# One written order of the seven products in the gate and up stage, with the fourth product cut in halves around the fifth

## The chip, the cores and the metric

The kernel runs on one core of one Trainium2 chip. The metric is device time in microseconds (us) of one execution of the whole program. TensorE multiplies, VectorE and ScalarE work element by element, and SyncE issues the DMAs. Each engine has its own list of instructions and takes them strictly in the order of that list; a semaphore makes an instruction wait for one of another engine.

## The reference, cut to what matters

The reference is one inference step of a one-layer decoder: input projection, windowed attention and pooling, output projection with a layer norm, and a gated feed-forward part. The change touches the gate and up products of the last part alone:

```python
def post_sublayers(h, attn_out, pool_out, w_o, ln1_g, ln1_b, w_gate, w_up, w_down, ln2_g, ln2_b):
    mix = jnp.einsum('bte,ed->btd', jnp.concatenate([attn_out, pool_out], -1), w_o)
    h1 = layer_norm(DEEPNORM_ALPHA * h + mix, ln1_g, ln1_b)
    a = jax.nn.silu(jnp.einsum('btd,df->btf', h1, w_gate)) * jnp.einsum('btd,df->btf', h1, w_up)
    ff = jnp.einsum('btf,fd->btd', a, w_down)
    return layer_norm(DEEPNORM_ALPHA * h1 + ff, ln2_g, ln2_b)
```

All is float32. There are 520 tokens here (8 sample rows and 512 prompt rows), 2048 model columns and 5632 feed-forward columns, which are 44 tiles of 128.

## The kernel before

**Seven products for a pair of tiles.** The gate and up stage works on 22 pairs of feed-forward tiles, and for each pair first on the gate weights (the "gate set", `g8` for pair 8), then on the up weights (the "up set", `u8`). A set has four raw weight tiles of 128x1024: two feed-forward tiles by two halves of the model columns. The 2x2 block product is done with seven products in place of eight (a Strassen-Winograd scheme). Products 1, 2 and 4 take a raw tile as it is; 7, 6, 5 and 3 take a *weight sum*, made in place by VectorE (line 196, one operation over 128x1024). The sums follow from each other: that for P6 needs the one for P7, those for P5 and P3 need the one for P6.

**Halves.** float32 precision is made of two float32r operands. Each 128x1024 tile is cut into two *halves* of 512 columns (P4a and P4b are the halves of P4). For each half `split` makes a *high part* (a cast on ScalarE, line 187) and a *low part* (a subtraction on VectorE, line 188). Then TensorE does 12 matmuls of 128x260 for it: four blocks of 128 columns, by three matmuls each (lines 203 and 204 read the high part, line 206 the low part). A full product is 24 matmuls.

**The ring.** High and low parts lie in two rings of five slots (`WB = 5`, line 46, set in line 810). Slots are given out in the order in which the code calls `split`: a half takes the slot of the half that was written five calls earlier, and its cast waits until TensorE has read that one.

**Accumulators.** P1, P6, P5 and P3 add up in one PSUM bank (`p1_g8`, `al` in the code), P7 and P4 in a second (`p7_g8`, `ga`), P2 has a third (`p2_g8`, `de`). Between the products of a bank its running value is copied out or added to the output rows (lines 1018 to 1054), and the next product on that bank waits for that reader.

**Filled, kept and other sets.** In ten early up sets (u1 to u11 without u5) P1 has been made beforehand, outside of the ring ("filled", `p1`). In g0 and u0 both P1 and P2 have been made ("kept"). All other sets do seven products. The written order in `run` (lines 1007 to 1061) depends on this: filled sets write P7, P2, P6, P4, P5, P3; kept ones P7, P6, P4, P5, P3; the others P1, P7, P6, P2, P5, P4, P3.

**What sets the order on the engines.** A scheduling pass of the framework places every instruction by its dependences, priorities and its own estimate of times; the written order decides which slot of the ring and which raw tile a half gets, and is the pass's starting point, but it does not fix the order on an engine. `weight_sum` (line 193) adds one fixed edge: a sum stands on VectorE behind the low part that was written last. The raw tiles (line 177) come by DMA from SyncE into six slots, each load as soon as the last reader of the slot is done. While gate set i runs, the results of pair i-1 are prepared for the next stage by `staged` (lines 1091 to 1116: four adds and eight casts and subtractions, with DMAs to `t_d`); `next(side)` places its pieces between the products.

Of the kernel before, what the change touches and what calls it, by code (L numbers as in the profile page):

```python
# [67 lines left out]
def hybrid_step(ctx, tc, xin, w_in, w_o, w_g, w_u, w_d, w_pool, par_d, cst_d, ident_d, ln2gb, kct_d, vc_d, hist_d,  # L68
                ck_d, cv_d, sp_d, yp, ys, nkp, nvp, npp, nks, nvs, nps):
    nc = tc.nc  # L70
# [5 lines left out]
    class Region:  # L76

        def __init__(self, name, dt, w):
            self.t, self.dt, self.spare = sb.tile([P, w], dt, name=name), dt, [(0, w)]
# [72 lines left out]
    def row_tile(name, w=NTOK):  # L152

        return ap_.tile([P, NTOK], F32, tag="row", name=name, bufs=bufs["row"])[:, :w]
# [28 lines left out]
    def split(s, name, lo=None):  # L183

        wh, wl = [sp[0].tile(list(s.shape), F32R, tag=t, bufs=sp[1]) for t in ("wh", "wl")]
        with tc.high_priority(prio[0]):
            nc.scalar.copy(wh, s)  # L187
            last_lo[0] = (lo or nc.vector).tensor_sub(wl, s, wh.bitcast(F32)).ins  # L188
        return wh, wl
# [10 lines left out]
    def products(out, wh, wl, hi, lo, first, last, onto=False):  # L200

        for j, o in enumerate(out):
            nc.tensor.matmul(o, wh, hi[j], start=first, stop=False, skip_group_check=onto)  # L203
            nc.tensor.matmul(o, wh, lo[j], start=False, stop=False, skip_group_check=onto)  # L204
        for j, o in enumerate(out):
            nc.tensor.matmul(o, wl, hi[j], start=False, stop=last, skip_group_check=onto)  # L206
# [48 lines left out]
    with ExitStack() as sa:  # L255
# [185 lines left out]
        for h in range(2):  # L441
            for g in range(4):
                n = h * 4 + g + 1
# [244 lines left out]
        def sample_attention():  # L688
# [10 lines left out]
            nc.scalar.copy(sT.rearrange("p j n -> p (j n)"), st_.rearrange("p j t b -> p (j t b)"))  # L699
            prod = pa.tile([P, 8, NS], F32, tag="smp", name="prod")  # L700
            nc.vector.tensor_add(prod, qd[:, 0], qd[:, 1])
            for i in range(2):
                ts = slice(4 * i, 4 * i + 4)
# [111 lines left out]
    def bank(name, w=HN):  # L815
        return ps.tile([P, 512], F32, tag="bank", name=name, bufs=banks)[:, :w]
# [130 lines left out]
    class Set:  # L947


        def __init__(self, w, i, name):  # L950
            self.w, self.i, self.name = w, i, name
            self.raw, self.bk, self.p1, self.s3, self.next = {}, {}, None, False, None

        def q(self, r, c):
            if (r, c) not in self.raw:
# [10 lines left out]
            self.s((1, 0), (0, 0), (1, 0), nc.vector.tensor_sub)  # L966
            self.s3 = True

        def prod(self, n, bk, first=True):


            b = {1: "b11", 2: "b21", 3: "b22", 4: "t4", 5: "t1", 6: "t2", 7: "t3"}[n]
            src = {1: lambda: self.q(0, 0), 2: lambda: self.q(0, 1), 4: lambda: self.q(1, 1),
                   7: lambda: self.q(1, 0) if self.s3 else self.s((1, 0), (0, 0), (1, 0), nc.vector.tensor_sub),
                   6: lambda: self.s((1, 0), (1, 1), (1, 0), nc.vector.tensor_sub),
                   5: lambda: self.s((0, 0), (1, 0), (0, 0), nc.vector.tensor_add),
                   3: lambda: self.s((0, 1), (0, 1), (1, 0), nc.vector.tensor_sub)}[n]()
            for g in range(2):
                wh, wl = split(src[:, g * 512:(g + 1) * 512], f"{self.name}_{n}{g}")
                if g == 0 and n == 1:  # L980
                    self.early()
                if g == 0 and n == 3 and self.next and (self.next.p1 is not None or self.next.bk):

                    self.next.early()
                for kk in range(4):
                    k = 4 * g + kk
                    sl = slice(kk * P, (kk + 1) * P)
                    hi, lo = bop[b][k // 2]
                    products([bk], wh[:, sl], wl[:, sl], [hi[:, k % 2, :]], [lo[:, k % 2, :]], k == 0 and first, k == 7, True)
# [17 lines left out]
        def run(self, c11, c12, c21, c22, side=(), out=None):  # L1007

            side = iter(side)
            r = row_tile(f"p_{self.name}")  # L1010
            filled = self.p1 is not None
            al, de = [self.bk.get(n) for n in (1, 2)]
            if not filled:
                self.p1 = r[:, HALF[0]]
                if al is None:
                    al = bank(f"p1_{self.name}")
                    self.prod(1, al)
                nc.scalar.copy(self.p1, al)
            else:
                al = bank(f"p1_{self.name}")  # L1020
            ga = bank(f"p7_{self.name}")
            next(side, None)
            self.prod(7, ga)
            next(side, None)
            kept = de is not None
            if filled and not kept:
                de = bank(f"p2_{self.name}")
                self.prod(2, de)
            if filled:
                nc.vector.tensor_add(c22, ga, self.p1)  # L1030
            else:
                nc.scalar.copy(c22, ga)
            self.prod(6, al, filled)
            next(side, None)
            if filled:
                nc.vector.tensor_add(c21, al, self.p1)
            else:
                nc.scalar.copy(c21, al)
            if filled or kept:
                self.prod(4, ga, False)  # L1040
            else:
                de = bank(f"p2_{self.name}")
                self.prod(2, de)
            next(side, None)
            nc.vector.tensor_add(c11, de, self.p1)
            if out:
                out(0)
            self.prod(5, al, False)
            next(side, None)
            nc.vector.tensor_add(c22, c22, al)  # L1050
            if not (filled or kept):
                self.prod(4, ga, False)
            next(side, None)
            nc.vector.tensor_add(c21, c21, ga)
            if out:
                out(1)
            self.prod(3, al, False)
            if filled:
                nc.vector.tensor_add(c12, al, self.p1)
                return c12  # L1060
            return al
# [68 lines left out]
    for j, s in enumerate(sets[NKEEP + 1::2][:NFILL]):  # L1130
        if j % 2 == 0:
            f = pb.tile([P, 2, HN], F32, tag="fill", name=f"fill{j}", bufs=NF)
# [82 lines left out]
    def column_pair(c, j):  # L1215

        A = {(r, b): wd[c, j, r, b] for r in range(2) for b in range(2)}
        tri = ps.tile([P, 3, 512], F32, tag="tri", name=f"tri{c}_{j}", bufs=2)[:, :, :HN]
        ga, de, al = [tri[:, i, :] for i in range(3)]
        ac = acc4[j]  # L1220
        if c == 0:
            for r in range(2):
                h = ac[:, 2 * r:2 * r + 2, :]
                nc.scalar.activation(h, h, AF.Copy, scale=ALPHA)

        def prod(n, bk, src, first=True):
            wh, wl = split(src, f"d{c}_{j}_{n}")
            for k in range(KP):
                hi, lo = ops[c][n][k][:, 0, :], ops[c][n][k][:, 1, :]
                products([bk], wh[:, k, :], wl[:, k, :], [hi], [lo], k == 0 and first, k == KP - 1, True)  # L1230

        def add(t, a, b, op):
            weight_sum(op, A[t], A[a], A[b])
            return A[t]


        prod(1, al, A[0, 0])
        yield
# [25 lines left out]
    g, before = [column_pair(0, j) for j in range(2)]  # L1264
# [5 lines left out]
    for x, (c, j) in enumerate(pairs[2:], 2):  # L1270
        g = column_pair(c, j)
# [4 lines left out]
        for i in range(5):  # L1276
# [7 lines left out]
            elif j < 2 * len(PLAIN) and i == 0:  # L1284
# [3 lines left out]
                f = j  # L1288
# [233 lines left out]
```

## Time and profile before

The three timed runs took 1931.68, 1930.22 and 1931.51 us. The page of the profiled execution gives its span and no other time of it.

| what | value |
|---|---|
| median of three runs | 1931.51 us |
| span of the profiled execution | 1931.1 us |
| mean granted TensorE clock | 0.992 |
| gate and up stage, 591 to 1449 us | 858.0 us, TensorE busy 850.15, VectorE 732.52, ScalarE 446.45, DMA share 0.49 |
| down stage, first part, 1449 to 1865 us | 416.0 us, TensorE busy 411.84, VectorE 348.27, ScalarE 172.63, DMA share 0.57 |

The stages' numbers come from the view of busy time by stretch. In the rows PE is TensorE, PEld its weight loads, DVE is VectorE, ACT is ScalarE, SPq the queue of SyncE. In a group's row stand the line, the engine, the operation, what is written and read, the count, the busy time with the mean of one, and the idle time ahead of it with what ended most of it. In the view by time a row gives the start in us, the duration in us and, in brackets, how long the engine was idle and who released it. Matmul records have a duration of 0.28 us but start every 0.12 us, since they are pipelined; starts are what to read there.

### The profile page before, as it was taken

How to read it: one execution, taken by the hardware profiler on the slowest of the kernel's cores; microseconds unless marked ns; L12 is line 12 of the kernel's file. 1: busy time of each engine (PE TensorE's matmuls, PEld its weight loads, DVE VectorE, ACT ScalarE, POOL GpSimd, SP SyncE). 2: the span in 40 equal slices, each digit the busy share in tenths (PEclk: the TensorE clock that was granted, in tenths of full speed). 3: DMA queues.
4: the chain of work that ended last, by engine and by line, in shares of the span. 5: the costliest groups of instructions: out<-in, count | busy, mean ns of one | idle time of the engine just before them, and what ended most of it. 6: DMA issues, size and time to landing. Idle time of an engine off the chain costs nothing.

```text
span 1931.1 us, 39334 instructions
## 1 busy us (share of the span) xinstructions
PE 1894.4 (98%) x15533; PEld 1865.8 (97%) x15533; DVE 1539.9 (80%) x2734; ACT 944.1 (49%) x1808; POOL 2.7 (0%) x9
## 2 busy tenths in 40 slices
PE   9999999999999999999999999999999999999996
PEld 8999999999989999999999999999999999999996
DVE  6666667768777888888888888888877888888878
ACT  6644445545654544554455555555554444344341
POOL 0000000000000000000000000000000000000000
PEclk9999999999999999999999999999999999999998
DMA  8732222665744555454545445454469664645332
GB/s 276 233 101 66 71 78 75 211 202 193 250 150 164 160 160 172 142 162 158 175 139 178 141 138 165 146 167 145 164 212 356 214 221 162 223 163 202 94 99 89
DMA packets 145241, 319.28 MB, mean 165 GB/s; under 512 B 14288, under 2 KB 66232, under 8 KB 144952
## 3 DMA queue, kind: packets, MB, share of 16 engines
q1 hardware_dynamic: 144480, 315.71, 49.7%
q8 instruction: 122, 2.00, 0.4%
q10 hardware_dynamic: 576, 1.05, 0.2%
q14 instruction: 63, 0.52, 0.1%
HBM read 265.22 MB, written 54.03 MB: 165 GB/s over the span
## 4 chain that ended last, share of the span: by engine, by line
PE 92%; DVE 4%; ACT 2%; DMA 1%; issue 1%; SPq 0%; DVEq 0%; ACTq 0%
PE p_g L203 7%; PE p_g L204 7%; PE p_g L206 7%; PE p_u L203 7%; PE p_u L206 7%; PE p_u L204 7%; PE tri L203 7%; PE tri L206 7%; PE tri L204 7%; PE o L203 3%; PE o L206 3%; PE o L204 3%; PE p_u L996 2%; PE mm_u L203 2%; PE mm_u L206 2%; PE mm_u L204 2%
## 5 line engine op out<-in xcount | busy, mean ns | idle before, releaser
L187 ACT CAST rr<-fr 128x512 fp32r<-128x512 f32 (+1 forms) x1056 | 658.0, 643 | 776.6 <-DVE fr L196 224.0
L188 DVE TENSOR_TENSOR rr<-fr,rr 128x512 fp32r<-128x512 f32 (+1 forms) x1056 | 738.0, 717 | 264.5 <-ACT rr L187 253.2
L196 DVE TENSOR_TENSOR fr<-fr 128x1024 f32<-128x1024 f32 (+1 forms) x304 | 319.7, 1052 | 5.8 <-DMA fr<-in_w_g_dram 5.0
L203 PE MATMUL p_g<-rr 128*128 128x260 f32 x830 | 235.5, 285 | 7.4 <-ACT rr L187 7.1
L206 PE MATMUL p_g<-rr 128*128 128x260 f32 x830 | 230.6, 282 | 0.0
L204 PE MATMUL p_g<-rr 128*128 128x260 f32 x788 | 221.8, 282 | 0.0
L203 PE MATMUL p_u<-rr 128*128 128x260 f32 x770 | 217.5, 283 | 0.2 <-ACT rr L187 0.2
L206 PE MATMUL p_u<-rr 128*128 128x260 f32 x770 | 215.3, 282 | 0.0
L204 PE MATMUL p_u<-rr 128*128 128x260 f32 x748 | 210.6, 282 | 0.0
L206 PE MATMUL tri<-rr 128*128 128x260 f32 x696 | 196.8, 283 | 1.5 <-DVE rr L188 1.5
L203 PE MATMUL tri<-rr 128*128 128x260 f32 x696 | 197.0, 283 | 0.7 <-ACT rr L187 0.7
L204 PE MATMUL tri<-rr 128*128 128x260 f32 x696 | 196.7, 283 | 0.0
L203 PEld LDWEIGHTS p_g<-rr 128*128 128x128 f32 x830 | 156.2, 188 | 9.9 <-ACT rr L187 9.4
L206 PEld LDWEIGHTS p_g<-rr 128*128 128x128 f32 x830 | 155.2, 189 | 0.0
L204 PEld LDWEIGHTS p_g<-rr 128*128 128x128 f32 x788 | 148.1, 188 | 0.0
L203 PE MATMUL o<-rr 128*128 128x260 f32 x512 | 145.0, 284 | 0.3 <-ACT rr L187 0.3
L203 PEld LDWEIGHTS p_u<-rr 128*128 128x128 f32 x770 | 144.9, 188 | 0.3 <-ACT rr L187 0.3
L206 PEld LDWEIGHTS p_u<-rr 128*128 128x128 f32 x770 | 144.6, 189 | 0.0
L204 PE MATMUL o<-rr 128*128 128x260 f32 x512 | 144.1, 282 | 0.0
L206 PE MATMUL o<-rr 128*128 128x260 f32 x512 | 143.6, 282 | 0.2 <-DVE rr L188 0.2
L204 PEld LDWEIGHTS p_u<-rr 128*128 128x128 f32 x748 | 140.6, 188 | 0.0
L206 PEld LDWEIGHTS tri<-rr 128*128 128x128 f32 x696 | 131.3, 189 | 2.2 <-DVE rr L188 2.2
(320 smaller groups left out, 4570.0 us busy)
## 6 DMA issues: line engine op xcount, KB each, us to landing
fr<-in_w_u_dram SPq DMA_DIRECT2D x100, 512.0 KB
fr<-in_w_g_dram SPq DMA_DIRECT2D x90, 512.0 KB
fr<-in_w_d_dram SPq DMA_DIRECT2D x64, 640.0 KB
t_d<-fr SPq DMA_DIRECT2D x140, 260.0 KB
fr<-in_w_o_dram SPq DMA_DIRECT2D x64, 512.0 KB
fr<-in_w_in_dram SPq DMA_DIRECT2D x48, 512.0 KB
rr<-t_d SPq DMA_DIRECT2D x87, 260.0 KB
mid_b<-t_d SPq DMA_DIRECT2D x53, 260.0 KB
```

Source lines behind the costliest of these rows:

```text
L187: nc.scalar.copy(wh, s)
L188: last_lo[0] = (lo or nc.vector).tensor_sub(wl, s, wh.bitcast(F32)).ins
L196: i = op(*args).ins
L203: nc.tensor.matmul(o, wh, hi[j], start=first, stop=False, skip_group_check=onto)
L204: nc.tensor.matmul(o, wh, lo[j], start=False, stop=False, skip_group_check=onto)
L206: nc.tensor.matmul(o, wl, hi[j], start=False, stop=last, skip_group_check=onto)
L996: nc.tensor.matmul(bk, self.q(0, n - 1)[:, k * P:(k + 1) * P], z1[0][4 * (n - 1) + k // 2][:, k % 2, :], start=(k == 0), stop=(k == 7))
```

## The change

`run` has one order for all sets: P1 (where it is not made beforehand), P7, P2, P6, the first half of P4, P5, the second half of P4, P3. `source(n)` gives a product's weights and makes the weight sum where one is needed, once; `prod` calls it, and `run` calls it for P5 ahead of P4a and for P3 ahead of P4b, so that these sums are written ahead of the halves. No instruction is added or dropped: the same matmuls, casts, subtractions, sums, adds and loads.

```diff
+        def source(self, n):
+            if n not in self.made:
+                self.made[n] = {
+                    1: lambda: self.q(0, 0), 2: lambda: self.q(0, 1), 4: lambda: self.q(1, 1),
...
+                    5: lambda: self.s((0, 0), (1, 0), (0, 0), nc.vector.tensor_add),
+                    3: lambda: self.s((0, 1), (0, 1), (1, 0), nc.vector.tensor_sub)}[n]()
+            return self.made[n]
+
+        def prod(self, n, bk, first=True, halves=(0, 1)):
...
-            for g in range(2):
+            src = self.source(n)
+            for g in halves:
                 wh, wl = split(src[:, g * 512:(g + 1) * 512], f"{self.name}_{n}{g}")
...
             self.prod(7, ga)
             next(side, None)
-            kept = de is not None
-            if filled and not kept:
+            if de is None:
                 de = bank(f"p2_{self.name}")
                 self.prod(2, de)
...
             self.prod(6, al, filled)
...
-            if filled or kept:
-                self.prod(4, ga, False)
-            else:
-                de = bank(f"p2_{self.name}")
-                self.prod(2, de)
+            self.source(5)
+            self.prod(4, ga, False, (0,))
             next(side, None)
             nc.vector.tensor_add(c11, de, self.p1)
             if out:
                 out(0)
             self.prod(5, al, False)
             next(side, None)
             nc.vector.tensor_add(c22, c22, al)
-            if not (filled or kept):
-                self.prod(4, ga, False)
+            self.source(3)
+            self.prod(4, ga, False, (1,))
             next(side, None)
             nc.vector.tensor_add(c21, c21, ga)
             if out:
                 out(1)
             self.prod(3, al, False)
```

What the scheduling pass makes of it is shown at three places of pair 8. Line numbers above 949 are larger by 3 to 7 in the changed file (1038 there is 1032 before, 1044 is 1038, 1053 is 1050, 1115 is 1112).

**First place: TensorE and ScalarE at P4 of g8.** On TensorE before, behind the last matmuls of P6 (bank `p1_g8`), two matmuls of P4a (bank `p7_g8`) stand ahead of P5 (again `p1_g8`); the other ten come after P5:

```order
L203 MATMUL p1_g8_9125<-rr_61 128x260
L204 MATMUL p1_g8_9125<-rr_61 128x260
L206 MATMUL p1_g8_9125<-rr_61 128x260
L203 MATMUL p7_g8_9158<-rr_61 128x260
L204 MATMUL p7_g8_9158<-rr_61 128x260
L203 MATMUL p1_g8_9125<-rr_61 128x260
L204 MATMUL p1_g8_9125<-rr_61 128x260
L206 MATMUL p1_g8_9125<-rr_61 128x260
```

On TensorE now, all twelve of P4a follow P6 at once, and two of P4b stand ahead of P5. These rows are the end of the twelve, the two, and the start of P5:

```order
L204 MATMUL p7_g8_9158<-rr_61 128x260
L206 MATMUL p7_g8_9158<-rr_61 128x260
L203 MATMUL p7_g8_9158<-rr_61 128x260
L204 MATMUL p7_g8_9158<-rr_61 128x260
L203 MATMUL p1_g8_9125<-rr_61 128x260
L204 MATMUL p1_g8_9125<-rr_61 128x260
L206 MATMUL p1_g8_9125<-rr_61 128x260
```

ScalarE before, from the copy of P1's result to that of P6's (line 1038). The casts of line 187 are those of P7b, P2b, P6a and P6b; then P4b and P5a; then P5b and P4a; then P3a:

```order
L1018 COPY fr_60<-p1_g8_9125 128x260
L187 CAST rr_61<-fr_60 128x512 x4
L1032 COPY fr_60<-p7_g8_9158 128x260
L187 CAST rr_61<-fr_60 128x512 x2
L1111 CAST fr_60<-fr_60 128x520
L187 CAST rr_61<-fr_60 128x512 x2
L1038 COPY fr_60<-p1_g8_9125 128x260
L187 CAST rr_61<-fr_60 128x512
```

ScalarE now, from the same copy of P1's result (line 1025). The casts are P6a, P6b and P4a; then P5a and P5b; then P4b; then P3a, P3b and the first three of u8:

```order
L1025 COPY fr_60<-p1_g8_9125 128x260
L187 CAST rr_61<-fr_60 128x512 x3
L1038 COPY fr_60<-p7_g8_9158 128x260
L1114 CAST fr_60<-fr_60 128x520
L187 CAST rr_61<-fr_60 128x512 x2
L1114 CAST fr_60<-fr_60 128x520
L187 CAST rr_61<-fr_60 128x512
L1070 ACTIVATE fr_60<-fr_60 128x260
L1044 COPY fr_60<-p1_g8_9125 128x260
L187 CAST rr_61<-fr_60 128x512 x5
```

P4a's cast moved from the second last of the set's middle to right behind P6's. Counted in the order of TensorE, P4a's slot was before that of P6b, the half directly ahead of it; now it is that of a half five places ahead.

**Second place: VectorE from P6 to P3 of g8.** Before, from P6b's low part (the first row; line 188 is a low part, 196 a sum, 1097 to 1112 are pieces of `staged`) up to the row ahead of the add that P3 waits for (line 1050). The sums are those for P3 and for P7 of u8; the one for P5 stands ahead of the piece:

```order
L188 TENSOR_TENSOR rr_61<-fr_60,rr_61 128x512
L1098 TENSOR_TENSOR fr_60<-fr_60 128x260
L188 TENSOR_TENSOR rr_61<-fr_60,rr_61 128x512
L196 TENSOR_TENSOR fr_60<-fr_60 128x1024
L188 TENSOR_TENSOR rr_61<-fr_60,rr_61 128x512
L1045 TENSOR_TENSOR fr_60<-p2_g8_9226,fr_60 128x260
L1101 TENSOR_TENSOR fr_60<-fr_60 128x260
L1112 TENSOR_TENSOR fr_60<-fr_60 128x520
L188 TENSOR_TENSOR rr_61<-fr_60,rr_61 128x512 x3
L196 TENSOR_TENSOR fr_60<-fr_60 128x1024
L1112 TENSOR_TENSOR fr_60<-fr_60 128x520
L188 TENSOR_TENSOR rr_61<-fr_60,rr_61 128x512
```

VectorE now, from P6b's low part on (the first row). The sums are those for P5, P3 and P7 of u8; the add of line 1053 that P3 waits for stands directly behind the last row:

```order
L188 TENSOR_TENSOR rr_61<-fr_60,rr_61 128x512
L196 TENSOR_TENSOR fr_60<-fr_60 128x1024
L188 TENSOR_TENSOR rr_61<-fr_60,rr_61 128x512
L1104 TENSOR_TENSOR fr_60<-fr_60 128x260
L1115 TENSOR_TENSOR fr_60<-fr_60 128x520
L1048 TENSOR_TENSOR fr_60<-p2_g8_9191,fr_60 128x260
L188 TENSOR_TENSOR rr_61<-fr_60,rr_61 128x512 x2
L196 TENSOR_TENSOR fr_60<-fr_60 128x1024
L1115 TENSOR_TENSOR fr_60<-fr_60 128x520
L188 TENSOR_TENSOR rr_61<-fr_60,rr_61 128x512 x2
L196 TENSOR_TENSOR fr_60<-fr_60 128x1024
L188 TENSOR_TENSOR rr_61<-fr_60,rr_61 128x512
```

P4a's low part moved ahead of P5's, P4b's behind the sum for P3, and the sum for P5 moved from ahead of P6a's low part to behind P6b's.

**Third place: VectorE at the start of g8.** Before, from the sum for P7 on (P1a's low part is the row ahead): P1b's low part, then the add on u7's bank (line 1050), then P7a's low part:

```order
L196 TENSOR_TENSOR fr_60<-fr_60 128x1024
L188 TENSOR_TENSOR rr_61<-fr_60,rr_61 128x512
L1050 TENSOR_TENSOR fr_60<-fr_60,p1_u7_8940 128x260
L188 TENSOR_TENSOR rr_61<-fr_60,rr_61 128x512
L1081 TENSOR_TENSOR fr_60<-fr_60 128x520
```

VectorE now:

```order
L188 TENSOR_TENSOR rr_61<-fr_60,rr_61 128x512
L196 TENSOR_TENSOR fr_60<-fr_60 128x1024
L1053 TENSOR_TENSOR fr_60<-fr_60,p1_u7_8940 128x260
L188 TENSOR_TENSOR rr_61<-fr_60,rr_61 128x512
L1084 TENSOR_TENSOR fr_60<-fr_60 128x520
```

The add on u7's bank moved ahead of P1b's low part. On TensorE P3 of u7, which waits for it, moved from behind P1 and two matmuls of P7 to behind P1a and two matmuls of P1b, 12 matmuls earlier.

More of the change, by code (lines that the diff above doesn't have):

```diff
@@ L951, in __init__ @@
             self.w, self.i, self.name = w, i, name
-            self.raw, self.bk, self.p1, self.s3, self.next = {}, {}, None, False, None
+            self.raw, self.bk, self.p1, self.s3, self.next, self.made = {}, {}, None, False, None, {}
         def q(self, r, c):
@@ L967, in early @@
             self.s3 = True
-        def prod(self, n, bk, first=True):
-            b = {1: "b11", 2: "b21", 3: "b22", 4: "t4", 5: "t1", 6: "t2", 7: "t3"}[n]
[L973 to L977, printed above, removed]
-            for g in range(2):
+        def source(self, n):
+            if n not in self.made:
+                self.made[n] = {
+                    1: lambda: self.q(0, 0), 2: lambda: self.q(0, 1), 4: lambda: self.q(1, 1),
+                    7: lambda: self.q(1, 0) if self.s3 else self.s((1, 0), (0, 0), (1, 0), nc.vector.tensor_sub),
+                    6: lambda: self.s((1, 0), (1, 1), (1, 0), nc.vector.tensor_sub),
+                    5: lambda: self.s((0, 0), (1, 0), (0, 0), nc.vector.tensor_add),
+                    3: lambda: self.s((0, 1), (0, 1), (1, 0), nc.vector.tensor_sub)}[n]()
+            return self.made[n]
+        def prod(self, n, bk, first=True, halves=(0, 1)):
+            b = {1: "b11", 2: "b21", 3: "b22", 4: "t4", 5: "t1", 6: "t2", 7: "t3"}[n]
+            src = self.source(n)
+            for g in halves:
                 wh, wl = split(src[:, g * 512:(g + 1) * 512], f"{self.name}_{n}{g}")
```

## The prediction

> **What bounds the kernel now.** First the page: its busy times, the shares of the chain that ended last, and the group of the stage that idles most (line, engine, operation; busy us and mean ns; idle us ahead of it).
>
> ```profile
> PE 1894.4 (98%) x15533; PEld 1865.8 (97%) x15533; DVE 1539.9 (80%) x2734; ACT 944.1 (49%) x1808; POOL 2.7 (0%) x9
> PE 92%; DVE 4%; ACT 2%; DMA 1%; issue 1%; SPq 0%; DVEq 0%; ACTq 0%
> L203 PE MATMUL p_g<-rr 128*128 128x260 f32 x830 | 235.5, 285 | 7.4 <-ACT rr L187 7.1
> ```
>
> TensorE is the bound, so time is only to be had from its idle gaps. Of those, the matmuls of the gate sets hold 7.4 us, nearly all ended by a cast. The same stage by stretches (start and end, length, busy time and instructions of TensorE, its weight loads, VectorE, ScalarE, GpSimd, then granted clock, DMA share, GB/s):
>
> ```profile
> 591.00:700.00 109.00, 107.42 (x889) 106.66 (x888) 92.30 (x144) 54.54 (x102) 0.00 (x0) 1.00 0.50 160
> 700.00:800.00 100.00, 98.07 (x812) 97.45 (x811) 87.46 (x142) 51.40 (x96) 0.00 (x0) 1.00 0.51 157
> 800.00:900.00 100.00, 98.55 (x817) 97.96 (x816) 87.74 (x142) 49.15 (x93) 0.00 (x0) 1.00 0.47 151
> 900.00:1000.00 100.00, 98.07 (x812) 97.45 (x811) 87.29 (x143) 50.39 (x95) 0.00 (x0) 1.00 0.53 166
> 1000.00:1100.00 100.00, 99.36 (x828) 99.15 (x828) 86.17 (x135) 53.70 (x101) 0.00 (x0) 1.00 0.48 154
> 1200.00:1300.00 100.00, 100.00 (x836) 100.00 (x835) 87.40 (x137) 54.31 (x103) 0.00 (x0) 1.00 0.50 158
> ```
>
> The last row is TensorE at its limit: 836 matmuls in 100 us, 0.1196 us from start to start (a half of 12 takes 1.435, a product 2.87). At that rate the 889, 812, 817, 812 and 828 matmuls of the first five rows need 106.3, 97.1, 97.7, 97.1 and 99.0 us. The stretches are longer by 2.65, 2.87, 2.27, 2.87 and 0.96: **11.6 us** in all. (A start-to-start count is used because a matmul's record of 0.28 us hides part of a gap.) Where it goes, in TensorE's rows by time in pair 8, the last matmul of P6b, the two of P4a, the first two of P5a:
>
> ```profile
> 862.38 0.28 PE L206 MATMUL p_g<-rr 128*128 128x260 f32 x1
> 863.31 0.39 PE L203 MATMUL p_g<-rr 128*128 128x260 f32 x1 [0.64 <-ACT rr L187]
> 863.53 0.28 PE L204 MATMUL p_g<-rr 128*128 128x260 f32 x1
> 863.65 0.32 PE L203 MATMUL p_g<-rr 128*128 128x260 f32 x1
> 863.81 0.28 PE L204 MATMUL p_g<-rr 128*128 128x260 f32 x1
> ```
>
> From 862.38 to 863.81 are four steps, 0.48 us at full rate, and 1.43 went by: 0.95 lost. ScalarE's rows say why:
>
> ```profile
> 861.19 0.62 ACT L187 CAST rr<-fr 128x512 fp32r<-128x512 f32 x1 [0.36 <-PE p_g L204]
> 862.63 0.62 ACT L187 CAST rr<-fr 128x512 fp32r<-128x512 f32 x1 [0.83 <-PE p_g L204]
> ```
>
> The second cast is P4a's. It stood idle 0.83 us until TensorE had read the slot's former half, and that half is P6b, directly ahead in TensorE's order. Two matmuls of P4a head the queue, so P5a, whose cast and low part were long done, waits behind them. The summary of what TensorE waits for between 591 and 1449 us counts 11 such waits (us in all, times, longest):
>
> ```profile
> PE p_g L203 <- ACT rr L187: 7.1, 11, 0.6
> PE p_g L203 <- ACT fr L1038: 0.3, 1, 0.3
> PE p_u L203 <- ACT rr L187: 0.2, 1, 0.2
> ```
>
> 11 × 0.95 = 10.4 of the 11.6 us. The rest, 1.2, is the other two rows and small steps.
>
> **The change: the bubble.** In the order now, P4a reuses the slot of a half five places ahead, P4b of one three places ahead, and the two matmuls pulled ahead of P5a are P4b's. No half of the changed file reuses the slot of the one directly ahead. With three places, the slot is free two halves (2.87 us) ahead of need, against a release to the cast of 0.25 (862.38 to 862.63), the cast's 0.62 and some 0.06 to the matmul. So all 11 bubbles go: −10.4. No instruction is added.
>
> **The other 1.2 us.** The largest is a VectorE add that P5 of an up set waits for (two rows of TensorE, one of VectorE):
>
> ```profile
> 844.74 0.28 PE L206 MATMUL p_u<-rr 128*128 128x260 f32 x1
> 845.19 0.36 PE L203 MATMUL p_u<-rr 128*128 128x260 f32 x1 [0.16 <-ACT rr L187]
> 844.62 0.42 DVE L1036 TENSOR_TENSOR fr<-p_u,fr 128x260 f32<-128x260 f32 x1
> ```
>
> The add ends at 845.04 and P5 starts 0.15 later: the bracket's cast is not the real releaser. Between P6 and P5 stands P4, as before, but the add has moved ahead of the piece of the stage's results; I count 0.8 us of room in place of 0.3 short. I take −1.2; the bounds are 0 and −1.2.
>
> **VectorE in a gate set.** It now carries the sums for P5 and P3 in the middle. Its prices:
>
> ```profile
> 860.67 1.22 DVE L196 TENSOR_TENSOR fr<-fr 128x1024 f32<-128x1024 f32 x1
> 861.81 0.69 DVE L188 TENSOR_TENSOR rr<-fr,rr 128x512 fp32r<-128x512 f32 x1
> 862.41 0.42 DVE L1045 TENSOR_TENSOR fr<-p_g,fr 128x260 f32<-128x260 f32 x1
> 862.75 0.42 DVE L1101 TENSOR_TENSOR fr<-fr 128x260 f32<-128x260 f32 x1
> 863.09 0.70 DVE L1112 TENSOR_TENSOR fr<-fr 128x520 fp32r<-128x520 f32 x1
> 863.70 1.90 DVE L188 TENSOR_TENSOR rr<-fr,rr 128x512 fp32r<-128x512 f32 x3
> ```
>
> From start to start a sum takes 1.14, a low part 0.60, a short add 0.34, a piece of 128x520 0.61. From P6a's low part to the end of the add that P3 waits for (line 1053) the order has eight low parts (4.8), three sums (3.4), three short adds (1.0), two pieces (1.2) and that add (0.42): 10.9, with the release 11.05. TensorE has 74 matmuls from P6's start to P3's, 8.85 us. So VectorE must be 2.2 us ahead when P6 starts. It can be: P2's last cast waits for TensorE to leave P3 of the set before, 58 matmuls (6.94) ahead of P6; a cast, a low part, a sum and three adds (0.62+0.60+1.14+1.02 = 3.4) leave a lead of 3.5. Margin 1.3, cost 0. With that cover gone, each missing 0.1 would cost 1.1 us in 11 sets.
>
> [...]
>
> **The tight place.** Behind each of the ten filled up sets, P3 moved forward, behind P1a and two matmuls of P1b of the next set, and its add waits on VectorE behind P1a's low part and a sum. Counted from the start T of P5a: P5a's last matmul starts at T+1.32, release 0.25 and cast 0.62 to T+2.19, low part to 2.79, sum to 3.93, add 0.42 and release 0.15 to **T+4.50**. TensorE reaches P3 after 38 matmuls, at **T+4.545**. The margin is nil. The row values scatter by a tenth, so I take 0.05 on average, 10 × 0.05 = +0.5; the bounds are 0 and 0.60 each (one low part placed in between), that is 0 and +6. In sets not filled ten more matmuls stand ahead of P3, and the margin is 1.2.
>
> **The load for P2 of an up set.** P2 now comes ahead of P6 there. SyncE's issue of its raw tile, and the cast that waited for it:
>
> ```profile
> 865.37 0.42 SPq L180 DMA_DIRECT2D fr<-in_w_u_dram  x1
> 871.63 1.14 ACT L187 CAST rr<-fr 128x512 fp32r<-128x512 f32 x2 [3.12 <-DMA fr<-in_w_u_dram]
> ```
>
> 6.26 us pass from issue to cast. The load waits for P5b's low part, now some 2.45 after P6's start in the gate set, in SyncE's order behind two stores as before but ahead of the other load it used to follow. First half cast by 2.45+6.26+0.62 = 9.3; use after 98 matmuls, 11.7. Hidden, by 2.4. If another transfer added over 2.4, each up set would pay the excess.
>
> **What stays.** A gap of 0.9 at the passage to the down stage stays: its cast waits for TensorE's own last reading.
>
> ```profile
> 1448.40 0.28 PE L206 MATMUL p_u<-rr 128*128 128x260 f32 x1
> 1449.43 0.39 PE L203 MATMUL tri<-rr 128*128 128x260 f32 x1 [0.74 <-ACT rr L187]
> ```
>
> Sum: −10.4 − 1.2 + 0.5 = −11.1. The profiled span, 1931.1, is 0.4 under the median of the runs, 1931.5, so the forecast is made against the latter: **1920.4 us**.
>
> **Rivals.** *Half given back.* In the tight place one VectorE operation too many, or its add regularly late by a low part: 10 × 0.60 = 6.0 returned, 1931.5−11.6+6.0 = 1925.9. For it: no margin; against it: the order has nothing else between.
>
> *The bubble only moves* (also: the change doesn't do what it says). The pass has again pulled two matmuls ahead of P5a, now P4b's, and the ring still has five slots. P4b's cast stands behind a piece on ScalarE (line 1114) that needs VectorE. If that cast is late by what P4a's was, 11 × 0.95 comes back: 1931.5−1.2 = 1930.3. For it: the same queue and the same two matmuls; against it: a slot free 2.87 us earlier. The Trainium skill, page "Perfetto Trace Analysis", section "Optimization Strategy", takes regular gaps of TensorE for too few buffers for the next tile. By that rule alone the unchanged ring would leave the gaps, and the time would be near this rival's; the trace agrees that a slot is what the cast waits for, but the stretch from 1200 us, on the same five slots, has none.
>
> *Slower: VectorE falls behind in the gate sets.* Before, VectorE had little lead at P6 of g8 (its start on P6a's low part, TensorE's first matmul of P6, and, in the view by stretches, the whole pair):
>
> ```profile
> 858.19 0.69 DVE L188 TENSOR_TENSOR rr<-fr,rr 128x512 fp32r<-128x512 f32 x1
> 858.43 0.28 PE L203 MATMUL p_g<-rr 128*128 128x260 f32 x1
> 846.00:884.40 38.40, 37.76 (x315) 37.55 (x314) 33.55 (x56) 19.36 (x37) 0.00 (x0) 1.00 0.50 160
> ```
>
> If the lead stays 0.24 where 2.2 is needed, P3 waits 1.96 in 11 sets: 21.6, and 1931.5−11.6+21.6 = 1941.5. It decides for slower at a lead under 0.8, where 11 × 1.4 outweighs 11.6 and the 3.9 of the bound below. For it: three sums in a row of work, and VectorE busy 33.55 of the pair's 38.40 us, 0.90 when the pair takes 37.4. Against it: a whole pair still fits, VectorE ran 87.40 in the 100 us of full rate above, and nothing in the order holds it back before P6 but the cast reckoned above.
>
> **How the numbers follow.** Forecast 0.66; half given back 0.16; bubble moves 0.10; slower 0.08. The low end is no cost in the tight place and a little of the last gap (1918.8). The high end takes in the second case, with the tight place at its bound and 0.6 unexplained: 1926.5. What is left out is the last two cases, 0.18. "Same" is within 0.2%, 3.9 us, about what a measurement of this kernel can tell: 1927.6 to 1935.4, and the third case lies in it. Faster 0.82, same 0.10, slower 0.08.
>
> **What would show it.** Right: between 591 and 1100 us TensorE makes close to 836 matmuls per 100 us; the row of 11 waits on line 187 by p_g is gone; P4a's cast no longer ends an idle time put down to TensorE. The tight place: a wait of p_u on line 203, with VectorE's line 1053 ending just ahead. Load: a wait of p_u for a cast that itself waited for in_w_u. Slower: p_g's P3 waiting, VectorE without idle time from P6 to P3. Wrong would be the whole sum if TensorE's gaps after P6 in gate sets are as long as before under another name.

## The result, and the profile after

| | median, us | runs | span of the profiled execution |
|---|---|---|---|
| before | 1931.6 | 4, 1930.22 to 1931.93 | 1931.1 |
| changed | 1922.42 | 4, 1920.50 to 1923.03 | 1921.2 |

The ratio is 0.995, with a 95% interval of 0.9939 to 0.9962: faster, by 9.2 us (7.3 to 11.8 by the interval). Inside the stage the profile shows more. The view of busy time by stretch of the changed kernel, in the columns of the prediction's table:

```profile
591.00:700.00 109.00, 109.00 (x909) 108.94 (x908) 94.56 (x149) 57.29 (x105) 0.00 (x0) 1.00 0.49 164
700.00:800.00 100.00, 100.00 (x836) 100.00 (x835) 89.99 (x146) 54.05 (x99) 0.00 (x0) 1.00 0.50 159
800.00:900.00 100.00, 100.00 (x837) 100.00 (x835) 88.80 (x146) 53.65 (x98) 0.00 (x0) 1.00 0.53 170
900.00:1000.00 100.00, 100.00 (x837) 100.00 (x836) 89.07 (x145) 52.32 (x95) 0.00 (x0) 1.00 0.49 159
1000.00:1100.00 100.00, 100.00 (x837) 100.00 (x837) 85.27 (x133) 56.74 (x104) 0.00 (x0) 1.00 0.46 154
```

TensorE makes 836 or 837 matmuls in each 100 us, the full rate. The summary of what it waited for between 591 and 1449 us, the row of eleven casts gone:

```profile
PE tri L203 <- ACT rr L187: 0.8, 1, 0.8
PE p_u L203 <- ACT fr L1044: 0.6, 1, 0.6
```

The first is the passage to the down stage, which stays. The second is new. How long the stage takes is read from TensorE's rows by time: its first matmul on `p_g` and the first of the down stage, before (the row at 1449.43 is in the prediction) and changed:

```profile
590.78 0.48 PE L203 MATMUL p_g<-mid_b,rr 128*128 128x260 f32 x1
```

```profile
591.23 0.48 PE L203 MATMUL p_g<-mid_b,rr 128*128 128x260 f32 x1
1438.77 0.39 PE L203 MATMUL tri<-rr 128*128 128x260 f32 x1 [0.75 <-ACT rr L187]
```

858.65 us have become 847.54, **11.1 less**. The span is only 9.9 shorter: 0.45 us were lost before the stage and 0.8 behind it, in code that the change doesn't touch. Both are small against how much these parts vary: over the profiles of all kernels here the stage starts between 589.4 and 591.6 us, and the part behind it takes 481.5 to 483.9 (e1 aside, where 24 matmuls of the stage run behind its end as counted here). Single runs of one kernel differ by 2.5 us here, and by up to 5 in the runs below.

### The profile page after: what moved, and what is told of

It reads as the page before. It is cut to its first block, busy times and chain, and to the rows that moved or that the text cites. A ratio compares the mean times of both kernels' runs of the same rounds, so it can differ in the third digit from the quotient of the medians.

```text
span 1921.2 us, 39215 instructions
## 1 busy us (share of the span) xinstructions
PE 1890.5 (98%) x15533; PEld 1862.9 (97%) x15533; DVE 1537.7 (80%) x2734; ACT 957.6 (50%) x1808; POOL 2.7 (0%) x9
## 4 chain that ended last, share of the span: by engine, by line
PE 92%; DVE 3%; DMA 2%; ACT 2%; issue 1%; SPq 0%; DVEq 0%; ACTq 0%
PE p_g L203 8%; PE p_g L204 8%; PE p_g L206 8%; PE p_u L203 7%; PE p_u L206 7%; PE p_u L204 7%; PE tri L203 6%; PE tri L206 6%; PE tri L204 6%; PE o L203 3%; PE o L206 3%; PE o L204 3%; PE p_u L1003 2%; PE mm_u L203 2%; PE mm_u L206 2%; PE mm_u L204 2%
## 5 line engine op out<-in xcount | busy, mean ns | idle before, releaser
L187 ACT CAST rr<-fr 128x512 fp32r<-128x512 f32 (+1 forms) x1056 | 669.9, 644 | 738.3 <-DVE fr L196 151.5
L196 DVE TENSOR_TENSOR fr<-fr 128x1024 f32<-128x1024 f32 (+1 forms) x304 | 319.2, 1050 | 4.9 <-DMA fr<-in_w_g_dram 4.3
```

The costliest lines, as they stand in the source:

```text
L196: i = op(*args).ins
```

## The experiments

**How the losses are counted.** A wait of TensorE is taken from start to start, less the 0.12 us of a normal step; the step behind a wait is 0.22 where a cast, a copy or a low part ended it, which adds 0.10, and 0.19 to 0.20 where an add did. For each kernel the ring was also counted in TensorE's written program: how many matmuls lie between the last reading of a slot's high part and the first matmul of the half that takes the slot. Before, this is 1 at eleven places (P4a of g1 to g4 and g6 to g12, in the slot of P6b). In the changed kernel it is nowhere under 13. The counts of the table come from that, not from a trace. Each ratio is to the kernel before as it ran in the same round, where its median was 1931.5 to 1932.3. The last column leaves out the passage to the down stage.

| kernel | median, us | ratio to before, 95% | closest slots | what TensorE waits for in the stage |
|---|---|---|---|---|
| e1 slot back | 1929.88 | 0.9981 to 0.9999 | 1, at 11 places | 11 casts |
| e2 slot away | 1940.37 | 1.0029 to 1.0054 | 1, at one place | 10 adds ahead of P3, 1 ahead of P5, 1 cast |
| e3 P2 ahead only | 1934.91 | 1.0006 to 1.0024 | 3, at one place | 12 adds ahead of P3, 1 cast |
| e4 filled and kept sets only | 1922.03 | 0.9935 to 0.9962 | 11, at 11 places | nothing |
| e5 P6 ahead | 1923.44 | 0.9943 to 0.9973 | none under 13 | 1 cast, for a load |
| e6 no sums ahead | 1934.43 | 1.0001 to 1.0019 | 3, at 9 places | 9 casts, 1 add |
| e7 P4 uncut | 1933.52 | 0.9998 to 1.0017 | none under 13 | 11 adds ahead of P3, 10 casts |
| e8 same order, slot free | 1929.80 | 0.9981 to 0.9999 | 11, at one place | 10 copies |
| e9 P5 behind P6 | 1944.02 | 1.0048 to 1.0075 | 1, at one place | 10 copies, 11 casts, 10 low parts |
| e10 sum for P5 ahead | 1934.16 | 1.0002 to 1.0020 | 3, at 9 places | 9 casts, 1 add |
| e11 sum for P3 ahead | 1920.61 | 0.9924 to 0.9951 | none under 13 | nothing |
| e12 copy not behind a cast | 1928.24 | 0.9968 to 0.9986 | none under 13 | 11 copies, 1 low part |

No version beats the changed kernel beyond the runs' spread; e4 and e11 equal it.

### What made the bubble: e1, e8, e12, e9

**e1.** In the changed kernel, ahead of the first half of P4:

```diff
+            if self.name in [f"g{i}" for i in (1, 2, 3, 4, 6, 7, 8, 9, 10, 11, 12)]:
+                for t in ("wh", "wl"):
+                    sp[0].rings[t][2] += 4
             self.prod(4, ga, False, (0,))
```

> The changed kernel, with P4a of the eleven gate sets that stalled before put back into the slot of P6b, the half directly ahead of it on TensorE; written order, cut and sums ahead stay. Slot theory: each of the eleven loses about 0.95 us again, 1922.4 + 10.4 = 1932.8 us, with 11 waits of about 0.6 us of p_g on line 203 for a cast. Rivals (the gain is from the sums written ahead, from the cut of P4, or from P2 ahead of P6): all of these are still there, so 1922.4 us and no such waits.

Measured: 1929.88 us, and in the summary of TensorE's waits the old row is back:

```profile
PE p_g L203 <- ACT rr L187: 7.1, 11, 0.6
```

Eleven waits of 0.95 as forecast; 1932.8 was too high by 3; of that 1.9 is the new wait at the end of u16 and the gap at the passage, which are not there in this kernel (0.86 and 1.03), and the rest is within what single runs differ by. But the slot did not act alone. With P4a late, the scheduling pass also put P5 back behind two matmuls of P4a, the order of before. So e1 shows that the slot brings the bubble; what the bubble consists of needs the next three.

**e8** leaves TensorE's order around P4 as before in ten of the eleven sets, and moves P4a's slot away by leaving four slots out ahead of P5:

```diff
+            if self.name in [f"g{i}" for i in (1, 2, 3, 4, 6, 7, 8, 9, 10, 11, 12)]:
+                for t in ("wh", "wl"):
+                    sp[0].rings[t][2] += 4
             self.prod(5, al, False)
```

> The kernel before with four slots of the ring left out ahead of P5 in the eleven gate sets. TensorE's order around P4 stays word for word (P6b, two matmuls of P4a, P5, the other ten, P4b), but P4a's slot is now that of P6a, read 12 matmuls earlier. Slot alone: all 10.4 us go, 1921.8 us. Slot and bank: P5a also waits for ScalarE's copy of P6's result out of its bank; counted from the start of P6b's last matmul 0.25 release, 0.37 copy, 0.12 to the matmul make 0.74, two matmuls cover 0.36, so 0.38 is left, 11 x 0.38 = 4.2 us: 1926 us, with 11 waits of p_g on line 203 for the copy of line 1038. Neither: 1932 us.

Measured: 1929.80. The cast waits are gone, and ten waits for the copy of line 1038 stand in their place, longer than expected. TensorE's and ScalarE's rows by time of e8 in g8 (last matmul of P6b, two of P4a, first of P5a; a cast and the copy):

```profile
860.89 0.28 PE L206 MATMUL p_g<-rr 128*128 128x260 f32 x1
861.01 0.28 PE L203 MATMUL p_g<-rr 128*128 128x260 f32 x1
861.13 0.28 PE L204 MATMUL p_g<-rr 128*128 128x260 f32 x1
862.09 0.39 PE L203 MATMUL p_g<-rr 128*128 128x260 f32 x1 [0.68 <-ACT fr L1038]
```

```profile
861.14 0.62 ACT L187 CAST rr<-fr 128x512 fp32r<-128x512 f32 x1 [0.50 <-PE p_g L204]
861.67 0.37 ACT L1038 COPY fr<-p_g 128x260 f32<-128x260 f32 x1
```

P4a's matmuls now run at once. P5a still loses 0.84 and 0.10: it adds onto the bank that P6 has just filled, and ScalarE must first copy P6's result out. The copy stands behind a cast, that of P4b, which now has P6b's slot and waits for it. The same is to be seen before: in ScalarE's rows there the copy ran behind P4a's cast,

```profile
863.16 0.37 ACT L1038 COPY fr<-p_g 128x260 f32<-128x260 f32 x1
```

to 863.53, and P5a started at 863.65. Its bank came free only 0.12 us ahead of that. In g1 of the kernel before, the copy was later still, and the trace names it as what P5a waited for:

```profile
633.04 0.39 PE L203 MATMUL p_g<-rr 128*128 128x260 f32 x1 [0.29 <-ACT fr L1038]
```

The eleventh set of e8 is a check on this: in g1 the scheduling pass put fourteen matmuls of P4 ahead of P5, and there P5a does not wait for the copy.

**e12** leaves one more slot out, so that P4b's cast is done early:

```diff
             for g in range(2):
+                if g and n == 4 and self.name in [f"g{i}" for i in (1, 2, 3, 4, 6, 7, 8, 9, 10, 11, 12)]:
+                    for t in ("wh", "wl"):
+                        sp[0].rings[t][2] += 1
                 wh, wl = split(src[:, g * 512:(g + 1) * 512], f"{self.name}_{n}{g}")
```

> The kernel of the run with the same order and a free slot, with one more slot left out ahead of P4b, so that P4b's cast no longer waits for P6b's slot in front of the copy on ScalarE. TensorE's order around P4 is still that of before. Slot and bank: only the copy itself is left, from the start of P6b's last matmul 0.25 + 0.37 + 0.12 = 0.74 us to P5a, of which P6b's own step and two matmuls of P4a cover 0.36, so 0.38 in each of the eleven, 4.2 us: about 1925 us, with waits of p_g on line 203 for the copy of line 1038 of about 0.1 to 0.2 us by the trace's count. Rival (P5a's start is set by something else behind P6, such as VectorE): as the run before it, 1929 to 1930 us.

Measured: 1928.24. TensorE's and ScalarE's rows at the same place:

```profile
859.74 0.28 PE L206 MATMUL p_g<-rr 128*128 128x260 f32 x1
859.86 0.28 PE L203 MATMUL p_g<-rr 128*128 128x260 f32 x1
859.98 0.28 PE L204 MATMUL p_g<-rr 128*128 128x260 f32 x1
860.49 0.39 PE L203 MATMUL p_g<-rr 128*128 128x260 f32 x1 [0.23 <-ACT fr L1041]
860.72 0.28 PE L204 MATMUL p_g<-rr 128*128 128x260 f32 x1
860.84 0.39 PE L206 MATMUL p_g<-rr 128*128 128x260 f32 x1
861.06 0.29 PE L203 MATMUL p_g<-rr 128*128 128x260 f32 x1
```

```profile
860.06 0.38 ACT L1041 COPY fr<-p_g 128x260 f32<-128x260 f32 x1 [0.88 <-PE p_g L206]
```

From P6b's last matmul to P5a are now 0.75 us (0.32 to the copy, 0.38 for it, 0.05 to the matmul), and the loss is 0.39 + 0.11 = 0.50 (0.38 expected, without the slow step), with another 0.10 at the third matmul. So with no cast waiting for a slot, 0.5 to 0.6 of the 0.95 of the bubble is left: that is the bank's copy with too little in front of it. The other 0.35 to 0.45 is the cast that waits for a slot and holds the copy up. 1925 us was missed by 3: besides the 0.1 to 0.2 in each set, three of the eleven sets lose more (0.83 at 1013.16, a low part at 632.94, and 0.29 at 937.08, for which the trace names no cause).

**e9** takes the two matmuls between P6 and P5 away. In the kernel before, in its P4 behind P5:

```diff
             if not (filled or kept):
+                if self.name in [f"g{i}" for i in (1, 2, 3, 4, 6, 7, 8, 9, 10, 11, 12)]:
+                    for t in ("wh", "wl"):
+                        sp[0].rings[t][2] += 3
                 self.prod(4, ga, False)
```

> The kernel before with three slots left out ahead of P4 in the eleven gate sets: on TensorE P5 then follows P6 at once, with nothing of P4 between, and no half in the gate sets follows directly on its slot's last (one in u12 does). Slot alone: 1922 to 1923 us. Slot and bank: P5a waits 0.25 + 0.37 + 0.12 - 0.12 = 0.62 us for the copy of line 1038 in each of the eleven, 6.8 us: 1928.5 to 1930 us.

Measured: 1944.02. The expected wait is there in ten sets; TensorE's rows by time of e9 show it in g8, from P6b's last matmul to P5a:

```profile
867.31 0.28 PE L206 MATMUL p_g<-rr 128*128 128x260 f32 x1
868.05 0.39 PE L203 MATMUL p_g<-rr 128*128 128x260 f32 x1 [0.47 <-ACT fr L1038]
```

0.74 from start to start, 0.62 lost, with the slow step 0.73. The remaining loss is from P4, which now comes late, and P3 right behind it waiting for a cast and low parts (0.39 and 0.55). For the question asked, the first wait is the answer: the bank alone costs this.

### Why the parts of the change hang together: e2, e3, e7

**e2**, the kernel before with one slot left out ahead of P4:

```diff
             if not (filled or kept):
+                if self.name in [f"g{i}" for i in (1, 2, 3, 4, 6, 7, 8, 9, 10, 11, 12)]:
+                    for t in ("wh", "wl"):
+                        sp[0].rings[t][2] += 1
                 self.prod(4, ga, False)
```

> The kernel before in its old written order, with one slot of the ring left out ahead of P4 in those eleven gate sets, so that P4a takes the slot of P2a and not of P6b. Slot theory: the eleven waits go, 1931.6 - 10.4 = 1921.2, and about 0.95 more where one half (P4a of u12) now follows directly on its slot's last: about 1922 us. Rivals: nothing of the new order is there, so 1931.6 us.

Measured: 1940.37, slower than before, against both. The eleven casts are gone, and the one expected at u12 is there. (The summary of waits names a cast twice more, at 636.72 and 847.99, but there a VectorE add ends 0.15 ahead of the matmul, so that it is the add.) But with P4a free early, the scheduling pass put all of P4 ahead of P5, and P3 now follows P5 on the same bank. TensorE's rows (last of P5b, first of P3a) and VectorE's:

```profile
870.96 0.28 PE L206 MATMUL p_g<-rr 128*128 128x260 f32 x1
872.74 0.36 PE L203 MATMUL p_g<-rr 128*128 128x260 f32 x1 [1.50 <-DVE fr L1050]
```

```profile
870.43 0.69 DVE L188 TENSOR_TENSOR rr<-fr,rr 128x512 fp32r<-128x512 f32 x1 [1.59 <-ACT rr L187]
871.04 1.22 DVE L196 TENSOR_TENSOR fr<-fr 128x1024 f32<-128x1024 f32 x1
872.18 0.42 DVE L1050 TENSOR_TENSOR fr<-fr,p_g 128x260 f32<-128x260 f32 x1
```

The add that takes P5's result stands behind a low part and a sum: 1.66 us lost in each of nine sets, 15. In a tenth, g1, it stands behind less and 0.77 is lost. That undoes the gain and more.

**e3**, P2 written ahead of P6 in the kernel before, and nothing else:

```diff
-            if filled and not kept:
+            if de is None:
                 de = bank(f"p2_{self.name}")
                 self.prod(2, de)
...
             if filled or kept:
                 self.prod(4, ga, False)
-            else:
-                de = bank(f"p2_{self.name}")
-                self.prod(2, de)
```

> The kernel before with one thing of the change: P2 written ahead of P6 in all sets; P4 uncut behind P5, no sum written ahead. P4a then has a slot three halves back, but P7a of eleven up sets, two matmuls of which stand ahead of P3 of the gate set, now takes the slot of P5b directly ahead. Slot theory: the loss only moves, 11 x 0.95 at P3 of the gate sets in place of P5, 1930 to 1932 us, with some 11 waits of about 0.6 us of p_u on line 203 for a cast. Rival (P2 ahead of P6 is what pays): 1920 to 1923 us.

Measured: 1934.91. The time is no gain, as the slot theory had it, but for another reason. Eleven matmuls, not one, lie between P5b's last reading and u8's P7a, since ten of P4b stand between; that covers nearly all; in u1, with three matmuls between, 1.31 is lost. The count by halves with which the expectation was written was too coarse, so e3's time is no support for it. The loss sits in twelve late sets, where P3 again follows P5 at once; TensorE's and VectorE's rows in u17:

```profile
1198.84 0.28 PE L206 MATMUL p_u<-rr 128*128 128x260 f32 x1
1199.73 0.36 PE L203 MATMUL p_u<-rr 128*128 128x260 f32 x1 [0.61 <-ACT rr L187]
```

```profile
1199.16 0.42 DVE L1047 TENSOR_TENSOR fr<-fr,p_u 128x260 f32<-128x260 f32 x1 [0.21 <-PE p_u L206]
```

The bracket names a cast; the add's end at 1199.58 and 0.15 more is the start, the same 0.15 as at 845.19 before. Here the add does not even stand behind anything, and 0.77 is lost.

**e7**, P4 whole ahead of P5:

```diff
             self.source(5)
-            self.prod(4, ga, False, (0,))
+            self.prod(4, ga, False)
...
-            self.source(3)
-            self.prod(4, ga, False, (1,))
```

> The changed kernel with P4 whole ahead of P5 (P7, P2, P6, P4, P5, P3), the sum for P5 ahead of it. No half follows directly on its slot's last. Slot theory: 1921 to 1924 us. Rival (the cut of P4 around P5 is what pays): 1926 to 1931 us.

Measured: 1933.52: the rival. In the summary of waits of e7 (the row of the add at the end of u16 left out):

```profile
PE p_g L203 <- DVE fr L1053: 3.4, 10, 0.6
PE p_u L203 <- ACT rr L187: 1.9, 10, 0.3
```

Two matmuls of the next P7 are all that lies between P5 and P3, and they wait for their cast (0.34 and 0.11 in g8) before P3 waits for its add (0.48 and 0.11): nine times 1.04, and somewhat more in g1. The cut puts ten matmuls of P4b there. In this order it is needed, not for the slot but for the bank.

### The sums, and the sets that need the order: e6, e10, e11, e4, e5

**e6** drops both calls of `source` from `run`, **e10** only the second, **e11** only the first:

```diff
-            self.source(5)
             self.prod(4, ga, False, (0,))
...
-            self.source(3)
             self.prod(4, ga, False, (1,))
```

> The changed kernel without the two calls that write the sums for P5 and P3 ahead of the halves of P4. No half follows directly on its slot's last. Slot theory: 1921 to 1924 us. Rival (the sums ahead are what pays): up to 1931 us, with TensorE waiting for low parts or casts of P5 and P3.

> The changed kernel with the sum for P5 written ahead and that for P3 not. Counted in TensorE's order, only three matmuls lie between the last reading of P4b and the first of u8's P2a, which takes its slot, at nine places, as in the run without both sums. Slot theory: nine waits of 1.15 us (start to start 1.43) of p_u on line 203, about 1934 us. Rival (both sums, through VectorE's load): half of it, 1928 us.

> The changed kernel with the sum for P3 written ahead and that for P5 not. No half has fewer than 13 matmuls between its first and the last reading of its slot. Slot theory: as the changed kernel, 1921 to 1924 us. Rival (both sums, through VectorE's load): 1928 us.

Measured: 1934.43, 1934.16 and 1920.61. The sum for P3 is needed, that for P5 is not. In e6 and e10 the sum for P3, and behind it that for P7 of the up set, come later on VectorE, and the scheduling pass puts the cast of u8's P2a ahead of that of its P7a. P2a has P4b's slot, and between them lie three matmuls. TensorE's rows of e6 (last two of P4b, first of u8's P7a) and ScalarE's, where the three casts are P2a, P7a and P7b:

```profile
867.39 0.28 PE L204 MATMUL p_g<-rr 128*128 128x260 f32 x1
867.51 0.28 PE L206 MATMUL p_g<-rr 128*128 128x260 f32 x1
868.94 0.39 PE L203 MATMUL p_u<-mid_b,rr 128*128 128x260 f32 x1 [1.15 <-ACT rr L187]
```

```profile
867.75 1.66 ACT L187 CAST rr<-fr 128x512 fp32r<-128x512 f32 x3 [2.46 <-PE p_g L204]
```

The first cast starts when P4b's slot has been read, and P7a's, which needs no such slot, has to follow it: 1.31 and 0.10 lost at nine places, 12.7 us. This is the slot's wait by itself, with no bank in it. e6's expectation had this wrong, because it was made with the count by halves; e10's and e11's were made with the count by matmuls, and hold.

**e4** keeps the old order in all sets that are neither filled nor kept; **e5** puts P6 ahead of P2 again in sets not filled. In e4 the switch is

```diff
+            plain = not filled and de is None
...
+            if plain:
+                de = bank(f"p2_{self.name}")
+                self.prod(2, de)
+            else:
+                self.source(5)
+                self.prod(4, ga, False, (0,))
...
+            if plain:
+                self.prod(4, ga, False)
+            else:
+                self.source(3)
+                self.prod(4, ga, False, (1,))
```

and in e5 P2 of the sets that are not filled moves behind P6:

```diff
-            if de is None:
+            if de is None and filled:
                 de = bank(f"p2_{self.name}")
                 self.prod(2, de)
...
+            if de is None:
+                de = bank(f"p2_{self.name}")
+                self.prod(2, de)
             self.source(5)
```

> The new order, cut and sums ahead in the filled and kept sets alone; all other sets (every gate set from g1 on) in the old order. Slot theory: P4a of the same eleven gate sets follows directly on its slot's last, so 11 waits as before and 1930 to 1932 us. Rival (the cut and the sums ahead in the filled up sets relieve VectorE ahead of the gate sets): under 1926 us.

> The changed kernel, but with P6 written ahead of P2 in the sets that are not filled, as before; cut and sums ahead stay. No half follows directly on its slot's last. Slot theory: 1921 to 1924 us, no row of eleven waits. Rival (P2 ahead of P6 is what pays): 1930 us or more.

Measured: 1922.03 and 1923.44. e4's expectation failed, again by the coarse count: P4a of g8 still has P6b's slot, but ten matmuls of P2b now stand between, so that its cast is done in time (ScalarE's row of e4; TensorE's first matmul of P4a is at 856.26):

```profile
855.21 0.62 ACT L187 CAST rr<-fr 128x512 fp32r<-128x512 f32 x1 [0.30 <-PE p_g L204]
856.26 0.28 PE L203 MATMUL p_g<-rr 128*128 128x260 f32 x1
```

The same ten cover the copy of P6's result. So the new written order in the filled up sets and the two kept sets is enough: the scheduling pass then places the products of the gate sets, unchanged in the code, differently. Why it does so stays open. P2 ahead of P6 is not needed either (e5; its one wait, 1.6 us at 639.38, is for a load of P2's raw tile).

## Why the prediction held, step by step

- **The bubble, −10.4.** All eleven went. The size was right; the account of it was half. "P5a, whose cast and low part were long done, waits behind them" left out that P5a's bank was copied out only at 863.53. Removing the slot's wait alone brought 1.7 us (e8), the cast in front of the copy too 3.8 (e12). The changed order removes both, since 14 matmuls of P4 now lie between P6 and P5. Its rows in g8 show it (TensorE's last matmul of P6b, first of P4a and first of P5a; ScalarE's copy):

```profile
856.00 0.28 PE L206 MATMUL p_g<-rr 128*128 128x260 f32 x1
856.12 0.28 PE L203 MATMUL p_g<-rr 128*128 128x260 f32 x1
857.79 0.28 PE L203 MATMUL p_g<-rr 128*128 128x260 f32 x1
```

```profile
856.32 0.38 ACT L1044 COPY fr<-p_g 128x260 f32<-128x260 f32 x1 [0.57 <-PE p_g L206]
```

  The copy starts 0.32 us behind P6b's last matmul and takes 0.38, as in e12, so it ends at 856.70, 1.09 us ahead of P5a.
- **The other 1.2.** Gone, with 845.19 among it. That add was not the largest of it, as the prediction has it (0.33 and 0.08): the copy that P5a of g1 waits for at 633.04 cost 0.46 and 0.10. It is the row of L1038 in the prediction's own summary of waits, and a sign, there before any run, of the bank that its account left out. Not foreseen was a new wait at the end of u16. ScalarE's and TensorE's rows of the changed kernel:

```profile
1429.85 0.64 ACT L1227 ACTIVATE fr<-fr 128x520 f32<-128x520 f32 x1 [2.17 <-DMA fr<-h_d]
1430.39 0.36 ACT L1044 COPY fr<-p_u 128x260 f32<-128x260 f32 x1
```

```profile
1430.80 0.39 PE L203 MATMUL p_u<-rr 128*128 128x260 f32 x1 [0.60 <-ACT fr L1044]
```

  A piece of the next stage that waits for a load stands ahead of the copy that P5 needs: 0.76 and 0.10. e4 and e11 have it not or smaller.
- **VectorE in a gate set, 0.** Right: the add ahead of P3 itself waits for TensorE in the changed kernel, so VectorE is ahead there. Of the 1.3 of margin, 0.34 and 0.66 are to be seen (the idle time in VectorE's row; its end at 861.30 and 0.15 more against P3 at 862.11):

```profile
860.87 0.43 DVE L1053 TENSOR_TENSOR fr<-fr,p_g 128x260 f32<-128x260 f32 x1 [0.34 <-PE p_g L206]
862.11 0.28 PE L203 MATMUL p_g<-rr 128*128 128x260 f32 x1
```

- **The tight place, +0.5.** It is as tight as reckoned, and costs nothing. VectorE's add and TensorE's first matmul of P3 of u7:

```profile
842.81 0.42 DVE L1053 TENSOR_TENSOR fr<-fr,p_u 128x260 f32<-128x260 f32 x1
843.39 0.28 PE L203 MATMUL p_u<-rr 128*128 128x260 f32 x1
```

  842.81 + 0.42 + 0.15 = 843.38, and P3 starts at 843.39, without the longer step that follows a wait. The same 0.16 to 0.17 from the add's end to P3 stands at all ten places: the scatter for which 0.05 was charged is not there.
- **The load, 0.** Right in the changed kernel, which has no such wait; e5 shows one.
- **The sum.** −11.1 in the stage was forecast and −11.1 measured. Part of that is luck: 0.5 was charged that did not come, and 0.86 came that was not charged. The waits that can be counted explain 10.7 of the 11.1. The time of the runs fell by 9.2, with an interval that takes in 11.1; the profile has the missing 1.2 outside the stage.
- **The rivals.** None happened in the changed kernel, but two did in its variants: the bubble moved in e6 and e10, and a late add ahead of P3 took the gain in e2, e3 and e7. The rule of the Trainium skill, page "Perfetto Trace Analysis", section "Optimization Strategy", that regular gaps can mean too little buffer space for the next tile, is half borne out: a slot was lacking at that place, but the same five slots do without a gap in another order.

## What to carry to other kernels

Count the distance of a ring slot, and of an accumulator's bank, in instructions of the engine that uses them, from the last use to the next first one: here some ten matmuls (1.2 us) between were enough for a slot's cast or a bank's copy, three were not. A gap with two late causes gives back little when one is removed (e8), so look for the second before counting the gain. The parts of an order hang together, and which of them carry it shows only when each is taken out: this one without its cut of P4, or without the sum for P3 ahead, was no faster than the kernel before, and P2 ahead of P6 by itself was slower; but without the sum for P5 ahead, without P2 ahead of P6, or with all sets that are neither filled nor kept in the old written order, it kept its gain.

## What was not expected of the hardware

A wait costs more than its length: behind every wait of 0.16 us or more in the stage, in all kernels here, the next step is 0.19 to 0.23 us in place of 0.12. From the start of a half's last matmul to ScalarE's copy out of its bank 0.32 us pass (e12, 859.74 to 860.06). To a cast that needs only a free slot it is 0.25 (862.38 to 862.63 before), but that cast is released by the last reading of the high part, one matmul earlier, and from there (862.26) it is 0.37. The tight place, with 0.01 to 0.02 us to spare, was met ten times of ten.
